# Delta rule block substitution on GpSimd, a new step order around it, and another timing model for the planned order

## The chip, the cores and the metric

One core of a Trainium2 chip runs the whole program in one launch. The metric is device time in microseconds (us), from the runs of the kernel on the chip; lower is better.

## What is computed

A two-layer model on 256 latent and 256 context tokens of width 1024. Each layer modulates its input, runs a mixer with three branches (a chunked delta rule, a gated linear attention and a differential attention), and a feed-forward part: dense in layer 0, a mixture of eight experts in layer 1. The change lies in the delta rule. Cut to it:

```python
decay = jnp.exp(jnp.where(incl, gc[..., :, None] - gc[..., None, :], -jnp.inf))
lmat = jnp.tril(jnp.einsum('bhnid,bhnjd->bhnij', kb, k) * decay, -1)
tinv = lax.linalg.triangular_solve(eye + lmat, eye, left_side=True, lower=True, unit_diagonal=True)
u = tinv @ (v * beta)
w = tinv @ (kb * jnp.exp(gc)[..., None])
# then a scan over the chunks: v_new = u - w @ s; s = s * gl + kg^T @ v_new
```

So for every head, direction and block of tokens a unit triangular matrix is inverted, and the scan over the chunks needs that inverse.

## The kernel before

The kernel is written tile by tile, in float32, with every large product made of three matmuls (lines 272 to 274) on operands split into two parts. A weight of 1 MB is fetched by SyncE into one of three buffers called raw; ScalarE casts its upper part (line 267), VectorE subtracts to get the lower part (line 268, two inputs from on-chip memory), and TensorE multiplies. Such a fetch with its two halves is one projection unit. Its two parts lie in a pool of six buffers (whl), its sums in three PSUM buffers (pm).

What runs in which order inside a mixer stands in PLAN, one line of short words per layer. The words that matter here: "pr" builds the triangular matrices U (a_prep), "iv" inverts them (a_inv and a_join), "sc" is the scan over the chunks (a_scan). "ga", "gb", "gc" with a number are that many gate projection units, stored to DRAM for later (gates_ahead); "za" is the two units of the output gate of the delta rule (z_ahead). "m" with a number runs so many steps of the modulation for later use (mod_unit): each fetches 1 MB of w_mod into raw and uses it in 16 small matmuls (line 348) without any work of VectorE or ScalarE on the weight. "qkB", "dec", "vB", "ha", "ma" are later steps of the other branches and of the merge.

Layer 1 works on half as many columns (256) in ga and za as layer 0 (512).

The inversion has three parts. First the diagonal blocks of 32 are gathered from U into one tile W and transposed (lines 638 to 648). Then comes the substitution: for c from 0 to 30 one multiplication (line 653) and one subtraction (line 655) on VectorE, over (31 - c) rows of (c + 1) elements on 128 partitions, each step reading what the step before wrote. At last the result is transposed back and put into U and a tile Q (lines 657 to 677), and a_join puts the blocks of 32 and 64 together with small matmuls (lines 699 to 728).

The word order in PLAN gives priorities, not the order on the engines. A planner in the tile framework works out an order for each engine from modelled durations, and every engine then takes its instructions strictly in that order.

Of the kernel before, what the change touches and what calls it, by code (L numbers as in the profile page):

```python
# [23 lines left out]
MOE_RAW = (1, 0, 0)  # L24
MOE_PART = 3
PRE = (7,)
PLAN = ("sm ap su pr iv ga4 m4 za sc m16 dec qkB gb1 ha ma vB gla qC kC m4 gc1 vC hb dif mb hc mc",
        "sm ap pr ga1 m8 iv sc za m6 ga3 m1 gc1 qkB dec vB ha ma gla qC kC m1 vC hb dif mb hc mc")
MOE_PRE = 9
MOE_AT = 0  # L30
PART = 512
# [165 lines left out]
class Prog:  # L197
# [430 lines left out]
    def a_inv(self, s):  # L628

        nc = self.nc  # L630
        U = s["U"]
        W1 = self.ch([2, 32, 32], "W1")
        W2 = self.ch([2, 32, 32], "W2")
        Dg, M, N, Y = W1[:, 0], W1[:, 1], W2[:, 0], W2[:, 1]
        nc.gpsimd.memset(Y, 0.0)
        nc.gpsimd.memset(Y.rearrange("p i j -> p (i j)")[:, 0:1024:33], 1.0)
        quad = [slice(b * 32, (b + 1) * 32) for b in range(4)]
        for d in range(2):
            for b, r in enumerate(quad):
                src, dst = U[d][r, :, r], Dg[r, :, 16 * d:16 * d + 16].rearrange("p i m -> p m i")  # L640
                if b % 2:
                    nc.vector.tensor_copy(dst, src)
                else:
                    nc.scalar.copy(dst, src)
        nc.vector.transpose(M, Dg)
        dmb = self.dmask[:, :, None].to_broadcast([128, 32, 32])
        nc.scalar.copy(N, M)
        nc.vector.copy_predicated(N, dmb, M.rearrange("p i j -> p j i"))
        for c in range(31):
            a, b = 31 - c, c + 1  # L650
            tmp = self.sm([512], "fs")
            tv = tmp[:, :a * b].rearrange("p (a b) -> p a b", a=a)
            nc.vector.tensor_mul(tv, N[:, c + 1:, c:c + 1].to_broadcast([128, a, b]),
                                 Y[:, c:c + 1, :b].to_broadcast([128, a, b]))
            nc.vector.tensor_sub(Y[:, c + 1:, :b], Y[:, c + 1:, :b], tv)
        Z, Ps, Qs = M, Dg, N
        nc.scalar.copy(Z, Y)
        nc.vector.copy_predicated(Z, dmb, Y.rearrange("p i j -> p j i"))
        nc.vector.transpose(Ps, Z)
        nc.vector.transpose(Qs, Z.rearrange("p i j -> p j i"))  # L660
        for d in range(2):
            for b, r in enumerate(quad):
                dst, src = U[d][r, :, r], Ps[r, :, 16 * d:16 * d + 16].rearrange("p i m -> p m i")
                if b % 2:
                    nc.vector.tensor_copy(dst, src)
                else:
                    nc.scalar.copy(dst, src)
        Q = W1.rearrange("p a i j -> p (a i j)").rearrange("p (d m j) -> p d m j", d=2, m=16)
        nc.gpsimd.memset(Q, 0.0)
        for d in range(2):  # L670
            for b, r in enumerate(quad):
                c = slice((b % 2) * 32, (b % 2) * 32 + 32)
                dst, src = Q[r, d, :, c], Qs[r, :, 16 * d:16 * d + 16].rearrange("p i m -> p m i")
                if b % 2:
                    nc.vector.tensor_copy(dst, src)
                else:
                    nc.scalar.copy(dst, src)
        self.a_join(U, Q)
# [761 lines left out]
    def mixer(self, l, H):  # L1440

        self.todo = self.mods(MOD_AHEAD[l], behind=0)
        T, m = {}, []
        gn = lambda n: self.P(f"gn{n}{l}") if n != "c" else self.A["gnc", l]
        zu = {"a": U_ZA, "b": U_RB, "c": None}
        for w in PLAN[l].split():
            if w == "su":
                self.setup2()
            elif w == "sm":
                self.small_proj(l, H)  # L1450
            elif w == "ap":
                self.a_proj(l, H)
            elif w == "pr":
                T["s"] = self.a_prep(l)
            elif w == "iv":
                self.a_inv(T["s"])
            elif w == "sc":
                T["oa"] = self.a_scan(l, T["s"])
            elif w == "qkB":
                T[w] = self.gla_qk(l, H)  # L1460
            elif w in ("vB", "vC"):
                T[w] = self.values(l, U_VB if w == "vB" else U_VC, H, w)
            elif w == "dec":
                self.gla_decays(l)
            elif w == "gla":
                T["ob"] = self.gla(l, T["qkB"], T["vB"])
            elif w == "qC":
                T[w] = self.diff_qk(l, H, w, U_QC, 256 * l, 0.125)
            elif w == "kC":
                T[w] = self.diff_qk(l, H, w, U_KC, 0, 1.0)  # L1470
            elif w == "dif":
                T["oc"] = self.diff(l, T["qC"], T["kC"], T["vC"])
            elif w[0] == "z":
                self.stashed[l, w] = self.z_ahead(l, zu[w[1]], H, gn(w[1]), w[1])
            elif w[0] == "g":
                self.gates_ahead(l, "abc".index(w[1]), H, int(w[2:] or 4))
            elif w[0] == "h":
                T["y" + w[1]] = self.head_out(l, T["o" + w[1]], gn(w[1]), H, zu[w[1]], w[1])
            elif w in ("ma", "mb", "mc"):
                first = not m  # L1480
                m = m or self.wide(l, "m")
                self.merge(l, "abc".index(w[1]), H, T["y" + w[1]], m, first)
            else:
                for _ in range(int(w[1:])):
                    next(self.todo, None)
        return m
# [86 lines left out]
```

## Time and profile before

| | us |
|---|---|
| median of 3 runs | 2604.94 (2601.87 to 2605.57) |
| profiled execution, its time | 2607.5 |
| profiled execution, its span | 2605.7 |
| TensorE busy | 2455.8 (94%) |
| VectorE busy | 1718.3 (66%) |
| ScalarE busy | 1417.3 (54%) |
| GpSimd busy | 87.6 (3%) |
| SyncE's transfers, busy share of the 16 DMA engines | 48.1% |

Engines in the rows below: PE is TensorE, PEld its weight loads, DVE VectorE, ACT ScalarE, POOL GpSimd, SP SyncE. Matmuls overlap, so the durations of single ones sum to more than the time that they take; the distance between starts is the time of one.

### The profile page before, as it was taken

Reading aid. Unit: us, or ns where it says so; the run is one execution under the profiler, and the core shown is the slowest. Engines: PE = TensorE matmul, PEld = TensorE weight load, DVE = VectorE, ACT = ScalarE, POOL = GpSimd, SP = SyncE. Lnnn points to the kernel's source line nnn. Section 1 sums busy time; section 2 is a strip of 40 time slices with the busy share of each in tenths; the row PEclk is TensorE's granted clock in tenths of the full one; section 3 lists DMA queues with packets and bytes.
Section 4 is the critical chain, followed back from the end, with each engine's and each line's share of the span. In section 5 each row is a group of like instructions: output and inputs, shape, how many; then the busy total and the mean of one; then the engine's idle time right before and its main releaser. Section 6 shows DMA issues by size and latency. Waiting matters only on the chain.

```text
span 2605.7 us, 35872 instructions
## 1 busy us (share of the span) xinstructions
PE 2455.8 (94%) x13712; PEld 1979.8 (76%) x13712; DVE 1718.3 (66%) x3130; ACT 1417.3 (54%) x2352; POOL 87.6 (3%) x216
## 2 busy tenths in 40 slices
PE   5998999999998999998979999998999999999997
PEld 3786777677677788886859878787878888878876
DVE  4675446655644533335686475767988888988987
ACT  3764343225553432334845432666878777777775
POOL 0000001110010000000000010010000000000000
PEclk8998999989999999998978999998999999999998
DMA  6323632022132223222273130246979899999994
GB/s 248 110 93 149 246 132 71 17 106 81 49 128 83 81 77 121 96 74 89 97 271 115 46 141 33 89 169 261 386 270 365 332 350 351 346 347 353 342 366 181
DMA packets 72707, 473.13 MB, mean 182 GB/s; under 512 B 8208, under 2 KB 10384, under 8 KB 19664
## 3 DMA queue, kind: packets, MB, share of 16 engines
q1 hardware_dynamic: 68208, 464.73, 48.1%
q10 hardware_dynamic: 4320, 6.03, 0.6%
q8 instruction: 110, 1.80, 0.3%
q14 instruction: 69, 0.57, 0.1%
HBM read 463.65 MB, written 7.08 MB: 181 GB/s over the span
## 4 chain that ended last, share of the span: by engine, by line
PE 85%; DVE 8%; ACT 4%; issue 2%; DMA 1%; SPq 0%; POOL 0%; ACTq 0%; DVEq 0%; POOLq 0%
PE pm L273 19%; PE pm L272 19%; PE pm L274 19%; PE y L274 3%; PE y L273 3%; PE y L272 3%; PE la L985 2%; PE pm L348 2%; PE pq L1052 1%; DVE ATb L987 1%; PE pm L844 1%; PE ob L996 1%; PE tp L1352 1%; DMA raw<-in_wmod_dram 1%; DVE zq L973 1%
## 5 line engine op out<-in xcount | busy, mean ns | idle before, releaser
L268 DVE TENSOR_TENSOR whl<-raw,whl 128x512 fp32r<-128x512 f32 (+2 forms) x490 | 331.2, 682 | 341.0 <-ACT whl L267 338.0
L272 PE MATMUL pm<-hh,whl 128*128 128x512 f32 (+2 forms) x1264 | 477.7, 380 | 13.0 <-ACT whl L267 6.6
L274 PE MATMUL pm<-hh,whl 128*128 128x512 f32 (+2 forms) x1264 | 467.7, 371 | 12.3 <-DVE whl L268 12.3
L267 ACT CAST whl<-raw 128x512 fp32r<-128x512 f32 (+2 forms) x490 | 289.8, 600 | 339.9 <-PE pm L274 268.7
L273 PE MATMUL pm<-hl,whl 128*128 128x512 f32 (+2 forms) x1264 | 470.9, 373 | 0.0
L268 DVE TENSOR_TENSOR wp<-rawc,wp 128x1024 fp32r<-128x1024 f32 x261 | 313.6, 1222 | 36.7 <-ACT wp L267 30.6
L272 PEld LDWEIGHTS pm<-hh,whl 128*128 128x128 f32 (+1 forms) x1264 | 244.8, 194 | 60.6 <-ACT whl L267 8.6
L274 PEld LDWEIGHTS pm<-hh,whl 128*128 128x128 f32 (+1 forms) x1264 | 243.5, 193 | 54.8 <-DVE whl L268 14.3
L267 ACT CAST wp<-rawc 128x1024 fp32r<-128x1024 f32 x261 | 268.1, 1051 | 21.1 <-PE y L274 11.5
L273 PEld LDWEIGHTS pm<-hl,whl 128*128 128x128 f32 (+1 forms) x1264 | 244.7, 194 | 42.6 <-issue 6.3
L268 DVE TENSOR_TENSOR wlo<-raw,whi 128x1024 fp32r<-128x1024 f32 x176 | 210.0, 1222 | 34.1 <-ACT whi L267 31.6
L273 PE MATMUL pm<-wlo,hg 128*128 128x512 f32 x530 | 211.8, 400 | 1.6 <-DVE wlo L268 1.4
L272 PE MATMUL pm<-whi,hg 128*128 128x512 f32 x530 | 211.2, 398 | 0.0
L274 PE MATMUL pm<-whi,hg 128*128 128x512 f32 x530 | 207.7, 392 | 0.0
L267 ACT CAST whi<-raw 128x1024 fp32r<-128x1024 f32 x176 | 179.0, 1052 | 13.2 <-PE pm L273 11.9
L273 PE MATMUL y<-wp,mt 128*128 128x512 f32 x348 | 135.4, 389 | 0.0
L274 PE MATMUL y<-wp,mt 128*128 128x512 f32 x348 | 135.3, 389 | 0.0
L273 PEld LDWEIGHTS pm<-wlo,hg 128*128 128x128 f32 x530 | 99.7, 188 | 34.6 <-DVE wlo L268 15.8
L272 PE MATMUL y<-wp,mt 128*128 128x512 f32 x348 | 120.1, 389 | 0.2 <-ACT mt L1354 0.2
L272 PEld LDWEIGHTS pm<-whi,hg 128*128 128x128 f32 x530 | 99.7, 188 | 20.9 <-ACT hg L1328 0.2
L274 PEld LDWEIGHTS pm<-whi,hg 128*128 128x128 f32 x530 | 99.7, 188 | 20.2
L268 DVE TENSOR_TENSOR wlo<-rawc,whi 128x1024 fp32r<-128x1024 f32 x91 | 110.9, 1219 | 1.9 <-ACT whi L267 1.3
(394 smaller groups left out, 4542.8 us busy)
## 6 DMA issues: line engine op xcount, KB each, us to landing
rawc<-in_m_dram SPq DMA_DIRECT2D x176, 1024.0 KB, 6.0
raw<-in_m_dram SPq DMA_DIRECT2D x88, 1024.0 KB, 7.4
raw<-in_win_dram SPq DMA_DIRECT2D x64, 1024.0 KB, 4.9
raw<-in_wmod_dram SPq DMA_DIRECT2D x40, 1024.0 KB, 5.0
raw<-in_f_dram SPq DMA_DIRECT2D x22, 1024.0 KB, 4.8
raw<-in_wo_dram SPq DMA_DIRECT2D x24, 512.0 KB, 3.7
raw<-in_f_dram SPq DMA_DIRECT2D x16, 704.0 KB, 4.0
rawc<-in_wmod_dram SPq DMA_DIRECT2D x8, 1024.0 KB, 16.9
```

Of the source, the lines that this page charges most:

```text
L267: self.nc.scalar.copy(hi, src)
L268: self.nc.vector.tensor_sub(lo, src, hi.bitcast(F32))
L272: mm(p, wh, ah, start=first, stop=False)
L273: mm(p, wh, al, start=False, stop=False)
L274: mm(p, wl, ah, start=False, stop=last)
L348: nc.tensor.matmul(p[j:j + 32, :256], self.cs[:, k, o:o + 32], w[:, k], start=i == 0 and k < 4, stop=i == n - 1 and k >= 4)
L844: nc.tensor.matmul(ps[:, :n], self.ones, sq[:, :n], start=True, stop=True)
L973: nc.vector.tensor_mul(FQ[hp][r, x, a].rearrange("p (n s) -> p n s", s=LEVELS[li]), side(Fj[:, x]), side(q[hp]))
L985: mm(p[:, x % 2, hp], FK[hp][:, x], FQ[hp][:, x], start=True, stop=True)
L987: nc.vector.copy_predicated(AT.rearrange("p h a (n t s) -> p (h a) n t s", t=2, s=s)[:, :, :, 1 - d], mk[:, None].to_broadcast([128, 4, 64 ...
L996: mm(o[:, hp], vB[:, tt, h * 128:(h + 1) * 128], AT[:, hp, a], start=True, stop=first)
L1052: mm(p[:, :nk], q[ms, h, cs], k[ms, h, :nk], start=True, stop=True)
```

## The change

The substitution's two instructions move from VectorE to GpSimd. The inversion is cut in two: a_inv ends with the substitution, and a new method a_blocks does the rest, from the copy that begins "Z" to the joins. A new word "jo" in PLAN calls it. PLAN is rewritten: in layer 0, "jo" stands behind "ga4 m4", with "za" behind it; in layer 1 "ga4 za m8" stands between "iv" and "jo", where "ga1 m8" stood ahead of "iv" and "za m6 ga3 m1" behind "sc", and the rest of the modulation ("m8") follows the scan; a last "m1" before "vC" goes. The tile context gets schedule_with_timeline_sim=True, so the planner works out its order with another timing model.

```diff
-PLAN = ("sm ap su pr iv ga4 m4 za sc m16 dec qkB gb1 ha ma vB gla qC kC m4 gc1 vC hb dif mb hc mc",
-        "sm ap pr ga1 m8 iv sc za m6 ga3 m1 gc1 qkB dec vB ha ma gla qC kC m1 vC hb dif mb hc mc")
+PLAN = ("sm ap su pr iv ga4 m4 jo za sc m16 dec qkB gb1 ha ma vB gla qC kC m4 gc1 vC hb dif mb hc mc",
+        "sm ap pr iv ga4 za m8 jo sc m8 gc1 qkB dec vB ha ma gla qC kC vC hb dif mb hc mc")
@@ a_inv
-            nc.vector.tensor_mul(tv, N[:, c + 1:, c:c + 1].to_broadcast([128, a, b]),
+            nc.gpsimd.tensor_mul(tv, N[:, c + 1:, c:c + 1].to_broadcast([128, a, b]),
                                  Y[:, c:c + 1, :b].to_broadcast([128, a, b]))
-            nc.vector.tensor_sub(Y[:, c + 1:, :b], Y[:, c + 1:, :b], tv)
-        Z, Ps, Qs = M, Dg, N
+            nc.gpsimd.tensor_sub(Y[:, c + 1:, :b], Y[:, c + 1:, :b], tv)
+        s["inv"] = W1, W2
+
+    def a_blocks(self, s):
+        U = s["U"]
+        W1, W2 = s["inv"]
+        Y = W2[:, 1]
+        Z, Ps, Qs = W1[:, 1], W1[:, 0], W2[:, 0]
         nc.scalar.copy(Z, Y)
         nc.vector.copy_predicated(Z, dmb, Y.rearrange("p i j -> p j i"))
@@ mixer
+            elif w == "jo":
+                self.a_blocks(T["s"])
@@ kernel
-    with tile.TileContext(nc) as tc:
+    with tile.TileContext(nc, schedule_with_timeline_sim=True) as tc:
```

## Rows read from the trace of the kernel before

**Rows 1.** The profile's page: span and instructions; busy time of each engine.

```profile
span 2605.7 us, 35872 instructions
...
PE 2455.8 (94%) x13712; PEld 1979.8 (76%) x13712; DVE 1718.3 (66%) x3130; ACT 1417.3 (54%) x2352; POOL 87.6 (3%) x216
```

**Rows 2.** Windows around both inversions: us, busy times, granted clock, DMA share, GB/s.

```profile
183.00:246.00 63.00, 49.99 (x652) 38.89 (x651) 44.30 (x100) 30.11 (x48) 1.81 (x1) 0.86 0.39 145
246.00:309.00 63.00, 62.23 (x615) 48.66 (x613) 25.22 (x54) 13.67 (x24) 0.00 (x0) 1.00 0.63 236
1302.00:1332.00 30.00, 22.77 (x225) 14.92 (x223) 23.85 (x79) 15.48 (x28) 0.00 (x0) 0.89 0.76 283
1302.00:1404.00 102.00, 80.92 (x1020) 65.54 (x1018) 81.47 (x201) 55.99 (x103) 1.81 (x1) 0.78 0.57 210
1404.00:1447.00 43.00, 43.00 (x362) 40.49 (x361) 19.75 (x40) 14.15 (x28) 0.00 (x0) 1.00 0.30 99
```

**Rows 3.** Windows of stages away from the inversions, the experts last.

```profile
400.00:580.00 180.00, 168.19 (x942) 128.91 (x940) 116.04 (x400) 51.50 (x118) 23.14 (x100) 0.94 0.17 63
620.00:740.00 120.00, 110.55 (x494) 75.97 (x493) 72.95 (x168) 66.92 (x147) 12.31 (x8) 0.97 0.21 75
1460.00:1600.00 140.00, 129.72 (x825) 105.69 (x825) 92.72 (x281) 59.72 (x138) 14.77 (x62) 0.99 0.25 87
1800.00:2580.00 780.00, 775.81 (x3550) 630.78 (x3550) 693.88 (x751) 591.47 (x738) 0.00 (x0) 1.00 0.90 341
```

**Rows 4.** Waits of PE, 1300 to 1420 us: total us, times, longest.

```profile
PE pm L348 <- DMA raw<-in_wmod_dram: 8.0, 6, 3.6
PE pm L274 <- DVE whl L268: 7.7, 2, 3.9
```

**Rows 5.** The substitution by source line: duration min/median/max ns, first and last start, forms.

```profile
L653 DVE TENSOR_TENSOR fs<-W x31: 192/360/425, 183.5 to 206.5; 128x31 f32<-128x31 f32 x2, 128x60 f32<-128x60 f32 x2, 128x87 f32<-128x87 f32 x2, 128x112 f32<-128x112 f32 x2
L655 DVE TENSOR_TENSOR W<-W,fs x31: 184/359/426, 183.8 to 207.2; 128x31 f32<-128x31 f32 x2, 128x60 f32<-128x60 f32 x2, 128x87 f32<-128x87 f32 x2, 128x112 f32<-128x112 f32 x2
L655 DVE TENSOR_TENSOR W<-W,fs x31: 183/359/424, 1339.2 to 1370.9; 128x31 f32<-128x31 f32 x2, 128x60 f32<-128x60 f32 x2, 128x87 f32<-128x87 f32 x2, 128x112 f32<-128x112 f32 x2
```

**Rows 6.** Two-input work on POOL: groups by shape, then single ones with DVE beside (timeline).

```profile
L1112 POOL TENSOR_TENSOR m<-m,sg 128x512 f32<-128x512 f32 x12 | 19.2, 1599 | 118.2 <-DVE sg L1111 92.5 <-DVE r L1059 19.7 <-DVE r L1054 6.0
L1112 POOL TENSOR_TENSOR m<-m,sg 128x256 f32<-128x256 f32 x14 | 13.5, 966 | 124.3 <-issue 63.1 <-DVE sg L1111 57.7 <-DVE r L1054 3.4
...
659.33 1.29 POOL L1112 TENSOR_TENSOR m<-m,sg 128x512 f32<-128x512 f32 x1 [19.71 <-DVE r L1059]
659.40 1.76 DVE L268 TENSOR_TENSOR whl<-raw,whl 128x512 fp32r<-128x512 f32 x1
...
1743.79 0.73 POOL L1112 TENSOR_TENSOR m<-m,sg 128x256 f32<-128x256 f32 x1 [5.47 <-DVE sg L1111]
```

**Rows 7.** Timeline of PE in layer 0: first join matmuls, first scan matmuls.

```profile
222.80 1.23 PE L699 MATMUL v<-W,U 32*32 32x32 f32 x116
...
246.35 1.05 PE L759 MATMUL V<-vtok,U 128*128 128x128 f32 x8
```

**Rows 8.** Layer 0: fetches behind "ga4", three modulation units on PE, one window of full DMA.

```profile
194.15 1.19 SPq L248 DMA_DIRECT2D raw<-in_win_dram  x2
200.18 0.33 SPq L248 DMA_DIRECT2D raw<-in_wmod_dram  x1
...
192.15 2.80 PE L348 MATMUL pm<-raw,cs 128*32 128x256 f32 x48
...
198.00:204.00 6.00, 3.69 (x22) 1.85 (x22) 5.52 (x15) 2.03 (x4) 0.00 (x0) 0.60 1.02 419
```

**Rows 9.** Pace of large matmuls: 512 columns (a window), 256 columns (two starts).

```profile
1060.00:1080.00 20.00, 20.00 (x90) 16.57 (x89) 8.16 (x12) 6.08 (x10) 0.00 (x0) 1.00 0.30 106
...
1341.17 0.28 PE L272 MATMUL pm<-hh,whl 128*128 128x256 f32 x1
1341.29 0.28 PE L273 MATMUL pm<-hl,whl 128*128 128x256 f32 x1
```

More of the change, by code (lines that the diff above doesn't have):

```diff
@@ L652, in a_inv @@
             tv = tmp[:, :a * b].rearrange("p (a b) -> p a b", a=a)
-            nc.vector.tensor_mul(tv, N[:, c + 1:, c:c + 1].to_broadcast([128, a, b]),
+            nc.gpsimd.tensor_mul(tv, N[:, c + 1:, c:c + 1].to_broadcast([128, a, b]),
                                  Y[:, c:c + 1, :b].to_broadcast([128, a, b]))
-            nc.vector.tensor_sub(Y[:, c + 1:, :b], Y[:, c + 1:, :b], tv)
-        Z, Ps, Qs = M, Dg, N
+            nc.gpsimd.tensor_sub(Y[:, c + 1:, :b], Y[:, c + 1:, :b], tv)
+        s["inv"] = W1, W2
+    def a_blocks(self, s):
+        nc = self.nc
+        U = s["U"]
+        W1, W2 = s["inv"]
+        quad = [slice(b * 32, (b + 1) * 32) for b in range(4)]
+        dmb = self.dmask[:, :, None].to_broadcast([128, 32, 32])
+        Y = W2[:, 1]
+        Z, Ps, Qs = W1[:, 1], W1[:, 0], W2[:, 0]
         nc.scalar.copy(Z, Y)
```

## The prediction

> **What bounds the kernel now.** I read the page first: PE is busy for 94% of the span and every other engine for much less [rows 1]. So time is to be had only where PE stands idle or runs slowly, and the next view is the windows over time. Around both inversions PE does both. In layer 0, from 183 to 246 us, it is busy 50.0 of 63 us (13.0 idle) at a mean granted clock of 0.86, which is the time at 2.4 GHz mixed with time at 1.2 GHz; 50.0 x 0.14 = 7 us more are lost to that. Together 20 us are lost. In layer 1, from 1302 to 1404, 21 us are idle and 80.9 x 0.22 = 18 us go to the clock: 39 us. Behind each, while the scan runs, PE is full at clock 1.00 [rows 2]. The third view is who PE waits for there: transfers of w_mod and the lower parts of weights (L268), which VectorE makes late because the substitution and the preparation stand ahead of them in its queue [rows 4]. So two things are late: DVE, and a DMA rate. A change here can win some part of 20 + 39 us, no more. Elsewhere the mixers' other branches leave 12, 9 and 10 us idle, and the experts 4 of 780 us [rows 3]: there is little to win there and much to lose.
>
> **The substitution on GpSimd.** Each layer has 31 steps of two instructions, together 2 x (sum of (31 - c)(c + 1)) = 2 x 5456 = 10,912 elements per partition. On VectorE it runs from 183.5 to 207.4 us in layer 0 (62 x 0.36 us by the medians, 22 us busy) and, mixed with other work, from 1338.5 to 1371.1 in layer 1 [rows 5]. On POOL the nearest rows are the merge's additions. The undisturbed ones take 1.29 us for 512 and 0.73 us for 256 elements, so 0.56 / 256 = 2.19 ns per element and 0.17 us per instruction; by that the chain takes 10,912 x 2.19 ns + 62 x 0.17 us = 34 us. The means, 1.599 and 0.966 us, give 2.47 ns and 0.33 us, so 27 + 21 = 48 us. Why the means are longer can be read too: a subtraction of a weight on VectorE that begins while an addition runs on POOL takes 1.76 us where its usual 0.69 would do, so the two engines hold each other up [rows 6]. In the changed kernel VectorE subtracts some 16 weight parts during the chain, and each can hold POOL up by about half its 0.69 us: 34 + 16 x 0.5 = 42 us. I take 42, with 34 and 48 as ends. That no row shows strided and broadcast operands on POOL is why 48 stays in the range. VectorE gets 22 us per layer back.
>
> The Trainium skill speaks against the step: "GPSIMD Engine Reference", section "Engine selection", sends elementwise work on two inputs to VectorE and calls GpSimd about twice as slow. By that factor 22 us become some 44 us (an estimate from that page), close to the sum from rows. What the rule leaves open is whether the lateness costs anything, and that is settled by what PE has to do meanwhile.
>
> **Layer 0.** The chain ends at 183.5 + 42 = 225.5 instead of 207.4. From there to the first full row of joins took 15.4 us, and from the joins to the scan 23.5 us, of which part was za's matmuls put between [rows 7]; without them I take 13. So joins begin at 241 and the scan at 254, 7.5 us later than before. What does PE do from 183 to 254? The end of ga4, 9 us (until the modulation at 192.15, as before). Then three waiting modulation units and a fourth, 4 us; the transfers for za are issued at 194 to 195 in either kernel and a 1 MB transfer needs 2.6 us at the 0.42 MB per us of the full window [rows 8], so about 7 us stay idle until 203. Now za can begin 4 us earlier, since its lower parts don't wait for the substitution: two units of 48 matmuls at 20 / 90 = 0.22 us [rows 9], 21 us, and 4 us for the clock to come back, until 228. From 228 to 241 only m16 is left, three units at hand and then one each 2.6 us for 1.0 us of PE: 6 us idle. Joins and scan start lose 3 more. Sum 7 + 4 + 6 + 3 = 20 us lost, as much as before: 0 gained. With a chain of 34 us it would be 5 gained, with 48 us 3 to 6 lost. What of m16 is done early, qkB's and gb1's 32 us of matmuls replace as cover of the scan.
>
> **Layer 1.** Ahead of "iv", ga4 takes the place of m8. Modulation needs nothing of VectorE; a gate unit needs four subtractions, 2.8 us, for 48 matmuls of 0.12 us = 5.6 us [rows 9]. While the preparation runs, VectorE has 6 of 30 us free [rows 2], so about two units fit and PE loses 4 us in place of 9.7 (7.2 idle, 2.5 clock). The chain starts at about 1335 (an estimate: 3 us earlier than now, with no modulation ahead of it) and ends at 1377; with the same 15.4 us and 11 us of joins the scan starts at 1404, as now. From 1332 the other four units of ga4 and za give PE 17 us at full pace (2 lost on the subtractions that POOL holds up). Then only modulation is left: about 36 us in which sixteen units at 2.6 us are fetched but give PE 17 us, so 19 us idle, and 4 us for the clock before gc1 and qkB arrive. Lost 4 + 2 + 19 + 4 = 29 against 39: 10 us gained. A chain of 34 us makes it 12, one of 48 us 7; 5 us either way for the guess of two units.
>
> **The order elsewhere.** Another timing model moves instructions in every stage. No row prices that, so it is bounded: below by half of the 31 us that the three mixed stretches leave idle, a gain of 15; above by the experts, which lose 0.5% now and might lose 3.5% (the mixed stretches lose 6.6 to 7.9% [rows 3]), a loss of 25. I take 0, since the experts' stretch is the longest and its loss is now the smallest.
>
> **Sum.** 0 + 10 + 0 from the profiled 2607.5 gives 2597.5; the median of the runs lies 2.6 below the profiled run, so **2595**.
>
> **The rivals.** *Slower: queues wait at the joins.* Engines take their instructions in planned order. If the planner holds POOL to be as fast as VectorE (24 us rather than 42), it puts the copy and the transposes behind the chain, and then the joins, 18 us too early, and VectorE, ScalarE and PE stand there with ready weights and za behind them. The price is the work that would have filled that time: about 13 us in layer 0 (za's end and six modulation units) and 9 in layer 1, so 2595 + 22 = 2617. It decides once the planned end lies more than about 10 us ahead of the real one. For it: today's order lets PE wait 7.7 us on weight parts that stand behind the substitution [rows 4], so the queues do block. Against it: the change brings a new timing model along, and a model that prices POOL long has no such loss.
>
> *No change: the idle time only moves.* Modulation stays bound by its transfers wherever it stands, and if only one gate unit fits into the preparation and the chain takes 48 us, layer 1 gains 2 and layer 0 loses 3: 2605.
>
> *Faster: the new order also helps elsewhere.* Chain of 34 us (5 + 12, and 5 for the units) and the 15 us: 2605 - 37 = 2568; half of the 15: 2575.
>
> **How the numbers follow.** My forecast has 0.42 (2584 to 2604 by itself), the waits at the joins 0.22, no change 0.14, the order helping 0.22. The range goes to the faster rival's far end, 2567, and upward to 2605 + 25 = 2630, which holds the slower rival too. A measurement of this kernel can tell some 0.2% (5 us) from no change. Of the forecast's chance 0.08 lies above 2600, so faster has 0.34 + 0.22 = 0.56, the same 0.20 (0.14 and 0.06), slower 0.24 (0.22 and 0.02).
>
> **What would show it.** The rows of lines 653 and 655 on POOL: first start to last end near 42 us in each layer; near 62 x 0.55 = 34 if VectorE doesn't disturb it. The windows 183 to 254 and 1302 to 1404: idle about 16 and 23 us. Weight parts of za made while the chain runs; if instead PE's wait before line 699 is one of over 8 us with line 272 behind it, the slower rival is right. The experts' 780 us should keep their length within 5 us; if they or the dense part move more, the order elsewhere decides, and my sum is wrong whatever the inversions show.

## The result and the profile after

The change makes the kernel slower: 2742.42 us (2738.34 to 2749.03, 4 runs) against 2604.07 (2601.87 to 2605.57) for the kernel before; the ratio is 1.0534, 95% interval 1.051 to 1.0559. That is 138 us more, on the other side of no change from the forecast and far outside its range. From about line 657 on, a line of the changed kernel has a number 10 higher than in the kernel before (the wait at 985 is now at 995).

The page of the changed kernel, its busy times and TensorE's granted clock in 40 slices:

```profile
span 2738.3 us, 36079 instructions
...
PE 2476.7 (90%) x13712; PEld 2022.1 (74%) x13712; DVE 1673.1 (61%) x3006; ACT 1420.5 (52%) x2352; POOL 156.7 (6%) x340
...
PE   6997889967969899999896889888999999999997
...
PEclk8998999966969999999996999799999999999998
```

Against [rows 1], TensorE runs the same 13712 matmuls and its busy time grew by 21 us, as more of them ran at the lower clock (the mean granted clock of the two executions is 0.962 and 0.928); its idle time grew from 150 to 262 us. VectorE was relieved by 45 us, GpSimd took on 69: the move itself did what it says. A slice is 68 us. The ninth, tenth and twelfth (548 to 684 and 753 to 821 us) have TensorE busy for 6, 7 and 6 tenths at a clock of 0.6: that is where layer 0's gated linear and differential attention run.

Windows of the changed kernel: both inversions, layer 1's substitution by itself, one stretch in the middle of layer 0's substitution, six windows at the end of layer 0's gated linear attention, and the experts (columns: length, busy time of PE, PEld, DVE, ACT and POOL with instruction counts, granted clock, DMA share, GB/s):

```profile
183.00:254.00 71.00, 50.27 (x673) 36.11 (x673) 28.94 (x41) 32.71 (x49) 37.13 (x63) 0.82 0.62 230
1400.00:1500.00 100.00, 76.05 (x848) 56.66 (x846) 53.57 (x123) 49.34 (x90) 34.08 (x63) 0.76 0.65 237
...
1437.40:1476.00 38.60, 24.77 (x208) 9.82 (x204) 1.60 (x8) 2.16 (x4) 32.28 (x62) 0.59 0.96 355
...
200.00:220.00 20.00, 20.00 (x87) 16.47 (x85) 6.88 (x8) 7.49 (x13) 18.04 (x26) 0.96 0.44 158
...
540.00:560.00 20.00, 15.44 (x107) 12.94 (x106) 12.11 (x38) 5.62 (x12) 2.02 (x10) 0.91 0.09 27
560.00:580.00 20.00, 13.78 (x52) 9.71 (x51) 7.72 (x27) 2.62 (x7) 2.02 (x8) 0.67 0.00 0
580.00:600.00 20.00, 12.40 (x43) 10.51 (x43) 10.53 (x40) 2.46 (x6) 2.55 (x11) 0.50 0.01 2
600.00:620.00 20.00, 13.83 (x56) 10.32 (x54) 10.15 (x44) 3.63 (x8) 2.61 (x12) 0.59 0.00 0
620.00:640.00 20.00, 13.50 (x42) 10.43 (x43) 8.33 (x30) 1.96 (x4) 2.12 (x9) 0.50 0.00 0
640.00:660.00 20.00, 15.37 (x51) 11.51 (x50) 7.88 (x26) 2.48 (x7) 1.01 (x4) 0.50 0.01 1
...
1920.00:2700.00 780.00, 767.99 (x3554) 631.91 (x3554) 682.89 (x747) 595.80 (x739) 0.00 (x0) 1.00 0.90 342
```

Read the line from 200 first: while GpSimd works on the substitution of layer 0 (18.04 of 20 us), TensorE is full, so the move is hidden there. In layer 1 it is not: from 1437 to 1476 us TensorE has 24.77 of 38.6 us at a clock of 0.59, the DMA engines are full (0.96), and its only work is modulation that waits for its transfers. Then the six windows from 540: no engine is full, next to nothing is fetched (DMA share 0.00 to 0.09), and from 560 us on TensorE works two thirds of the time (68.9 of 100 us) at a granted clock of 0.50 to 0.67; 0.50 is its lower level of 1.2 GHz. The same stage had 168 of 180 us at 0.94 before (400 to 580 us in [rows 3]). The experts' 780 us lose 12.0 instead of 4.2.

Waits of TensorE over the whole changed kernel (total us, times, longest) and the substitution by source line:

```profile
PE la L995 <- DVE Fe L986: 38.3, 16, 3.5
PE pm L348 <- DMA raw<-in_wmod_dram: 25.9, 15, 4.1
...
PE tp L1075 <- DVE e L1072: 22.8, 8, 4.3
```

```profile
L653 POOL TENSOR_TENSOR fs<-W x62: 238/547/1089, 190.7 to 1473.9; 128x31 f32<-128x31 f32 x4, 128x60 f32<-128x60 f32 x4, 128x87 f32<-128x87 f32 x4, 128x112 f32<-128x112 f32 x4
```

In the kernel before, the same three waits were these:

```profile
PE pm L348 <- DMA raw<-in_wmod_dram: 11.8, 7, 3.7
PE tp L1065 <- DVE e L1062: 6.8, 11, 1.1
...
PE la L985 <- DVE Fe L976: 6.4, 13, 1.0
```

The waits for Fe and for e belong to the gated linear attention and to the differential attention, whose code the change doesn't touch. What is new there is the planner's order; the experiments below take it by itself.

Where the time went can be followed by landmarks, the first or last start of one instruction each (us):

| landmark | before | after |
|---|---|---|
| first addition of scan outputs, layer 0 | 264.9 | 281.6 |
| first addition of gated linear attention outputs | 460.6 | 503.9 |
| first copy of differential attention outputs | 642.7 | 709.0 |
| last residual addition of the mixer, layer 0 | 835.6 | 923.6 |
| last addition of the dense part, layer 0 | 1211.1 | 1299.1 |
| last addition of scan outputs, layer 1 | 1449.8 | 1579.1 |
| last copy of differential attention outputs, layer 1 | 1700.2 | 1837.7 |

17 us are lost by the first scan, 27 from there to the second landmark, 23 to the third, 22 to the end of layer 0's mixer, none in the dense part, 41 to the end of layer 1's scan, and 8 to the last; in the profiled runs 5 come back behind it.

### The profile page after: what moved, and what is told of

Its sections match the earlier page's. It is cut to its first block, busy times and chain, and to the rows that moved or that the text cites. A ratio compares the mean times of both kernels' runs of the same rounds, so it can differ in the third digit from the quotient of the medians.

```text
span 2738.3 us, 36079 instructions
## 1 busy us (share of the span) xinstructions
PE 2476.7 (90%) x13712; PEld 2022.1 (74%) x13712; DVE 1673.1 (61%) x3006; ACT 1420.5 (52%) x2352; POOL 156.7 (6%) x340
## 5 line engine op out<-in xcount | busy, mean ns | idle before, releaser
L268 DVE TENSOR_TENSOR whl<-raw,whl 128x512 fp32r<-128x512 f32 (+2 forms) x490 | 337.1, 696 | 368.1 <-ACT whl L267 364.5
```

The costliest lines, as they stand in the source:

```text
L268: self.nc.vector.tensor_sub(lo, src, hi.bitcast(F32))
```

## Experiments

Times are medians; ratios are against runs of the kernel before on the same chip. "The model" is schedule_with_timeline_sim=True.

**The change in its parts.** Theory A: the model's order costs the time. Rival B: the substitution on GpSimd does. Four kernels take the parts one by one.

The kernel before with the model alone:

```diff
-    with tile.TileContext(nc) as tc:
+    with tile.TileContext(nc, schedule_with_timeline_sim=True) as tc:
```

> The kernel before with nothing changed but the timing model of the planner; substitution on VectorE and plan as before. Theory A (the order of the new timing model carries the loss): 2690 to 2740 us, with the linear attention of layer 0 ending in a stretch of over 60 us in which PE is half busy at a granted clock near 0.5. Rival B (the plan and the later joins carry it): within 10 us of the kernel before, 2595 to 2615 us.

Measured: 2725.89 (2724.93 to 2731.28), ratio 1.0467 (1.0442 to 1.0492): 119 of the 138 us with nothing moved to GpSimd. Its windows have the same hole; this is the stretch 500 to 640 us:

```profile
500.00:640.00 140.00, 109.18 (x552) 90.72 (x551) 68.91 (x240) 32.18 (x70) 14.79 (x64) 0.71 0.11 38
```

And so are the waits of TensorE for VectorE:

```profile
PE la L985 <- DVE Fe L976: 36.2, 17, 3.5
...
PE tp L1065 <- DVE e L1062: 23.8, 8, 4.3
```

The changed kernel without the model:

```diff
-    with tile.TileContext(nc, schedule_with_timeline_sim=True) as tc:
+    with tile.TileContext(nc) as tc:
```

> The changed kernel with the old timing model: substitution on GpSimd, joins as a step of their own, new plan. Theory A: 2580 to 2610 us, as the sum of the prediction without its term for the order (2595). Rival B (plan and later joins): 2700 us or more. A third reading, that the old model misjudges GpSimd and the queues wait at the joins: 2615 to 2640 us, with a wait of over 8 us ahead of the join matmuls.

The kernel before with only the two instructions on GpSimd, PLAN and model as before:

```diff
-            nc.vector.tensor_mul(tv, ...)
-            nc.vector.tensor_sub(Y[:, c + 1:, :b], ...)
+            nc.gpsimd.tensor_mul(tv, ...)
+            nc.gpsimd.tensor_sub(Y[:, c + 1:, :b], ...)
```

> The kernel before with only the substitution's two instructions moved to GpSimd; plan and timing model as before, joins directly behind the substitution. Theory A: within 15 us of the kernel before (the chain ends some 10 us later than on VectorE, VectorE is free meanwhile). Rival (queues wait at the joins): 2620 us or more.

Measured: 2645.05, ratio 1.015 (1.012 to 1.018), and 2645.46, ratio 1.0144 (1.0118 to 1.017). So GpSimd costs 38 us under the old model. One window of the first, then its wait of ScalarE; one window of the second, then its wait of TensorE in layer 1:

```profile
200.00:220.00 20.00, 0.00 (x0) 0.00 (x0) 0.00 (x0) 1.02 (x2) 16.52 (x32) 0.50 0.23 95
```

```profile
ACT W L667 <- POOL W L655: 52.6, 2, 26.3
```

```profile
200.00:220.00 20.00, 0.19 (x4) 0.00 (x0) 0.00 (x0) 0.00 (x0) 17.49 (x33) 0.50 0.31 129
```

```profile
PE v L699 <- ACT W L677: 28.4, 1, 28.4
```

For 20 us next to nothing runs but GpSimd. In the first kernel ScalarE has reached the first copy of the joins (line 667) and waits 26 us for it. In the second, layer 1, TensorE itself stands 28.4 us at the joins' first matmul, the sign that the prediction named. This is its "slower" rival, in the kernels without the model. In the changed kernel no queue stands like that: TensorE had 20.00 of 20 us in layer 0, and in layer 1 it waited for transfers.

The new PLAN and the split of a_inv alone, with the substitution on VectorE and the old model, against the changed kernel:

```diff
-            nc.gpsimd.tensor_mul(tv, ...)
-            nc.gpsimd.tensor_sub(Y[:, c + 1:, :b], ...)
+            nc.vector.tensor_mul(tv, ...)
+            nc.vector.tensor_sub(Y[:, c + 1:, :b], ...)
...
-    with tile.TileContext(nc, schedule_with_timeline_sim=True) as tc:
+    with tile.TileContext(nc) as tc:
```

> The kernel before with the new plan and the joins as a step of their own, the substitution still on VectorE, old timing model. Theory A: 2590 to 2615 us. Rival B (the plan carries the loss): 2700 us or more, since layer 1 has no gate units left for its scan.

Measured: 2609.21, ratio 1.0015 (1.0003 to 1.0027). PLAN costs some 3 us (1 to 7 by the interval). So A carries 119 us. B is worth 38 without the model and, by difference, some 16 with it (138 less 119 for the model and 3 for PLAN).

**What in the model's order?** First theory: independent projections are used up too early. In the changed kernel the three projections of the differential attention were done by 546 us, and the gated linear attention ran alone until 658.

The kernel with the model, with these projections held back behind steps of the gated linear attention:

```diff
+            at = {"qC": (0, 1, 0), "kC": (1, 0, 0), "m4": (1, 1, 0), "gc1": (1, 1, 0), "vC": (1, 1, 1)}.get(w)
+            with self.tc.issue_after(self.step[at]) if at else nullcontext():
                 self.item(l, w, H, T, m, gn, zu)
```

> The kernel before with the timing model alone (2726 us), with layer 0's independent projections held back on TensorE's queue to the pace of the gated linear attention: those of the differential attention's q behind its second step, of k behind the third, the modulation and gate behind the fourth, of v behind the fourth's second direction (in the kernel before they stood like that; with the model all of them were used up by 546 us, and from there to 640 us TensorE ran half busy at a clock of 0.50 to 0.59). Theory 'the model's order spends the independent work too early': the stretch 500 to 640 us has TensorE at 17 of 20 us or more per window and a clock over 0.8, and 25 to 35 us come back: 2690 to 2702 us. Rival 'the model's order of the recurrence itself is slower, on VectorE and ScalarE, and the projections have no part in it': the low windows only move, to 430 to 540 us or behind it, and the time stays within 10 us of 2726.

The same, and each part of layer 0's second merge behind one query tile of the differential attention:

```diff
         for pr in range(4):
+            at = l == 0 and j == 1 and self.dstep[l, pr]
+            with self.tc.issue_after(at) if at else nullcontext():
```

> As the kernel with the projections held back, and with the four parts of layer 0's second merge held back as well, one behind each query tile of the differential attention (with the model, TensorE was at 11 to 14 of 20 us at a clock of 0.54 to 0.74 from 760 to 820 us). Theory 'spent too early': another 15 to 20 us come back, 2670 to 2687 us. Rival 'the recurrence and the softmax themselves': no more than 5 us beside the kernel with the projections alone.

The changed kernel with both:

> The changed kernel (2742 us) with both held back in layer 0, the projections behind the gated linear attention's steps and the second merge's parts behind the query tiles. Theory 'spent too early': 40 to 55 us come back, 2687 to 2702 us, since its low windows (540 to 660, 760 to 820 us) are those of the kernel with the model alone. Rival 'the recurrence and the softmax themselves': within 10 us of 2742.

Measured: 2720.46 (ratio 1.0445, 1.0427 to 1.0462), 2710.96 (1.0402, 1.0377 to 1.0428), 2737.78 (1.051, 1.0492 to 1.0527). By the loss against the kernel before on the same chip 3, 13 and 5 us came back, where 25 to 55 were expected. The theory fell: the holes moved, as its rival said. The timeline of TensorE in the first of them shows how a step now runs (line 987 is 985 before; start us, length, engine, line, what, and in brackets idle time with its releaser):

```profile
495.38 1.19 PE L987 MATMUL la<-zq,Fe 128*128 128x128 f32 x4 [1.61 <-DVE Fe L978]
...
497.65 2.38 PE L987 MATMUL la<-zq,Fe 128*128 128x128 f32 x8
503.71 3.36 PE L987 MATMUL la<-zq,Fe 128*128 128x128 f32 x12 [3.68 <-DVE Fe L978]
508.73 0.77 PE L998 MATMUL ob<-ATb,vB 128*128 128x128 f32 x2 [1.66 <-DVE ATb L989]
...
517.08 0.63 PE L272 MATMUL pm<-hh,whl 128*128 128x512 f32 x1
```

And in the kernel before, at the same place in a step:

```profile
472.91 0.39 PE L274 MATMUL pm<-hh,whl 128*128 128x512 f32 x1
473.35 0.68 PE L985 MATMUL la<-zq,Fe 128*128 128x128 f32 x4
...
474.57 0.39 PE L272 MATMUL pm<-hh,whl 128*128 128x512 f32 x1
```

From 484 to 517 us no projection matmul (lines 272 to 274) runs; TensorE waits for VectorE, and its clock is 0.50, so that four products of 128 columns take 1.19 instead of 0.68 us. In the kernel before a step is shot through with projection matmuls. Counting, from the timelines of TensorE, the times of over 3 us in layer 0's gated linear attention (from its first decay matmul to the end of its last output) from the end of one projection matmul to the start of the next: before 8 of them, together 65 us, the longest 22; with the model 3, together 137, the longest 112; with the projections held back 6, together 140, the longest 50; in the changed kernel 3, together 137, the longest 112.

Second theory: blocks instead of weaving. The kernel with the model, with 144 groups of three projection matmuls woven by hand into the eight steps, and as a control the kernel before with the same:

```diff
+                        with self.pump(5):
                             for x, li in enumerate(ls):
...
+                        with self.pump(3):
                             for a, r in enumerate(rows):
```

Here pump(n) traces n groups behind TensorE's last instruction, and what stands under it is queued behind them.

> The kernel before with the timing model (2726 us), with layer 0's gated linear attention and its independent projections (q, k, v of the differential attention, one gate: 144 groups of three matmuls) woven together by hand: five groups are queued on TensorE between the matmuls that make the decay factors and the products that wait for them, three between the products and the outputs, in each of its eight steps. With the projections only held back by steps, the model's order still issued a step's own matmuls in one block (484 to 516 us: 32 us for one step, TensorE at a clock of 0.52 with holes of 1 to 4 us behind VectorE) and the projections in another; in the kernel before a step with projections in its holes took 23 us (466 to 489) at full clock. Theory 'blocks instead of weaving: the holes and the half clock that they bring': the stretch 380 to 640 us has TensorE at 17 of 20 or more and the clock at 0.9 or more, and 30 to 45 us come back, 2681 to 2696 us. Rival 'the model's order of the recurrence on VectorE and ScalarE': the holes stay beside the woven projections, 2710 us or more.

> The kernel before, with the planner's old model, and the same weaving by hand in layer 0's gated linear attention. By the weaving theory the old model wove by itself: nothing to win, 2600 to 2615 us. If the weaving by hand is itself a gain or a loss of more than 12 us, the reading of the kernel with the model has to be corrected by that.

Measured: 2770.72 (ratio 1.0633, 1.06 to 1.0666) and 2650.97 (1.017, 1.0138 to 1.0202). My fixed weave costs 46 us by itself, so by the rule set down ahead the reading is corrected by that: between the two kernels lie 120 us, as much as the model costs without the weave (119). Windows of the first and of the control, 380 to 680 us:

```profile
380.00:680.00 300.00, 251.29 (x1357) 207.68 (x1356) 141.74 (x447) 70.71 (x156) 24.12 (x104) 0.84 0.18 64
```

```profile
380.00:680.00 300.00, 270.63 (x1600) 223.53 (x1599) 165.59 (x507) 98.37 (x221) 25.90 (x105) 0.95 0.19 68
```

In these 300 us TensorE gets 1357 instructions done with the model, and 1600 without; but the control ends its gated linear attention at 612 us and goes on to other work, the first kernel only at 676. From its first decay matmul to that end the stage takes 313 us with the model and 264 without. So with equal weave the model still costs 49 us there: the place of the projections is not all of it, and something else in the order has a part.

**Whose order?** That question can be put without a theory of the order. The kernel is planned once with the old model, and TensorE's instructions are then held in just that order (an edge from each to the next) while the model plans the other engines; and the complement.

```diff
+    _, per = build(False)
+    nc, _ = build(True, [per[e] for e in ENGINES])   # each list: o[n] issued behind o[n-1]
...
+ENGINES = ('PE',)      # the complement: ('DVE', 'Activation', 'Pool', 'SP')
```

> The kernel before with the timing model (2726 us), but TensorE's instructions are held in the very order that they have in the kernel before; the model plans VectorE, ScalarE, GpSimd and the fetches around that. Theory 'TensorE's order decides' (projections and recurrence in the wrong turn): 2604 to 2630 us. Rival 'the order on VectorE and ScalarE decides' (each waits behind other work while TensorE stands): 2690 us or more. Between: both have a part.

> The complement: VectorE, ScalarE, GpSimd and the fetches are held in the order of the kernel before, and the model plans TensorE alone. Theory 'TensorE's order decides': 2680 us or more. Rival 'the order on VectorE and ScalarE decides': 2604 to 2640 us.

Measured: 2638.84 (ratio 1.0134, 1.0109 to 1.0159) and 2792.0 (1.0714, 1.0697 to 1.0732). TensorE's order brings back 85 of the 119 us; 34 stay, more than expected. Without TensorE's order, the old order of all others is of no use, and worse than none (+68). In the gated linear attention of the first one:

```profile
355.00:600.00 245.00, 215.70 (x1198) 169.50 (x1198) 144.97 (x458) 72.86 (x160) 25.80 (x112) 0.94 0.20 74
```

The stage takes 248 us (353 to 601), against 235 before and 289 with the model alone; its times without a projection are 9, together 68 us, the longest 24. Of the 34 us that stay, 18 are lost by the first copy of differential attention outputs in layer 0, 4 from there to the end of layer 1's scan, and 15 to the last copy; 4 come back behind it. TensorE, in its old order, waits more for the two other engines:

```profile
PE la L985 <- DVE Fe L976: 27.4, 26, 1.9
...
PE v L699 <- ACT W L677: 17.0, 2, 9.6
```

Before, these two were 6.4 and 1.2 us. So what is left agrees with a worse order on VectorE and ScalarE.

**What makes the queues stand still without the model?** First try: cover is missing. The joins are queued on TensorE, VectorE and ScalarE behind the last gate (layer 0) or behind za (layer 1):

```diff
+                for i in pins: es.enter_context(self.tc.issue_after(i))
                 self.a_blocks(T["s"])
...
+            if w == ("ga4", "za")[l]: pins = [last instruction of each engine]
```

> The changed kernel with the planner's old model (2645 us, 15 of whose first 20 us after the chain's start at 200 us had TensorE, VectorE and ScalarE all waiting for GpSimd), and one thing more: everything of the joins on TensorE, VectorE and ScalarE is queued behind the last instruction of the gates (layer 0) or of the delta rule's z (layer 1) on the same engine, so that no queue can reach the joins before some 35 to 42 us of projections have been issued. Theory 'the standstill is the whole price of GpSimd under the old model': TensorE is full from 200 to 220 us and from 1360 to 1390 us, 30 to 45 us come back, 2597 to 2615 us, about the kernel before or a little under it. Rival 'the chain on GpSimd costs elsewhere too (its instructions hold VectorE up, the order around it is worse)': TensorE is full there, but the time stays over 2625 us.

Measured: 2640.44, ratio 1.0141 (1.0124 to 1.0159); TensorE 0.89 of 20 us from 200 to 220. Nothing was cured, since the pins held the joins behind the wrong thing. I first read it as gates issued too early, and held the cover itself back, on TensorE behind the last matmul ahead of the chain ("[" to "]" in PLAN), with the joins behind the cover:

```diff
+PLAN = ("... iv ga4 [ za gb1 ] m4 jo sc m16 dec qkB ha ...",
+        "... iv ga2 m4 [ ga2 za gc1 ] m4 jo sc m8 qkB ...")
```

> The changed kernel's parts with the planner's old model (2645 us), with cover that is queued on TensorE between the chain on GpSimd and the joins: behind the last matmul ahead of the chain stand the delta rule's z and a gate of the gated linear attention (layer 0: some 32 us of projections), or two gates, z and another gate (layer 1: some 27 us), and everything of the joins on TensorE, VectorE and ScalarE stands behind those. With the joins queued behind the gates alone the standstill stayed (TensorE 0.89 of 20 us from 200 to 220), because the gates were issued ahead of the chain. Theory 'the standstill is the whole price of GpSimd under the old model': TensorE is nearly full through both chains and 30 to 45 us come back, 2595 to 2615 us. Rival 'work held for the chain is missing ahead of it or behind it': the holes only move, to the preparation ahead of the chain or the scan behind it, and the time is over 2625 us.

Measured: 2606.29 (2601.82 to 2611.16, 10 runs), ratio 1.0004 (0.9989 to 1.002): the 38 us came back. Layer 0's chain is covered, layer 1's not (windows), and the timeline of layer 1 tells what the wait is:

```profile
200.00:220.00 20.00, 20.00 (x90) 16.57 (x89) 6.07 (x7) 9.14 (x15) 17.88 (x28) 1.00 0.44 151
...
1360.00:1380.00 20.00, 0.42 (x4) 0.00 (x0) 7.26 (x7) 5.24 (x5) 9.80 (x22) 0.50 0.30 114
```

```profile
1371.48 1.04 ACT L667 COPY W<-W 128x1024 f32<-128x1024 f32 x1 [17.88 <-POOL W L655]
...
1380.06 0.37 ACT L356 COPY modr<-pm 128x256 f32<-128x256 f32 x1
...
1380.48 1.02 PE L359 MATMUL pm<-cstt,modr 128*128 128x8 f32 x4 [20.06 <-ACT modr L356]
```

A copy of 0.37 us that has nothing to do with the inversion, the modulation's (line 356), stands on ScalarE behind the joins' first copy (line 667). That one waits for GpSimd, and TensorE waits 20.1 us for the small copy, with all its other work behind. The timeline of TensorE in the changed kernel without the model has the same wait in layer 0:

```profile
197.05 1.07 PE L348 MATMUL pm<-raw,cs 128*32 128x256 f32 x16 [3.72 <-DMA raw<-in_wmod_dram]
220.35 1.02 PE L359 MATMUL pm<-cstt,modr 128*128 128x8 f32 x4 [22.23 <-ACT modr L356]
```

So in these two places TensorE stood neither at the joins' matmuls nor for want of work, but at a place in a queue. The direct trial holds nothing back for the chain, and only queues the joins behind all that PLAN sets ahead of them, za and the modulation included:

```diff
+PLAN = ("... iv ga4 m4 za } jo sc m16 ...", "... iv ga4 za m8 } jo sc m8 ...")
...
+            if w == "}": pins = [last instruction of TensorE, VectorE, ScalarE]
```

> The changed kernel with the planner's old model (2645 us), with the joins on TensorE, VectorE and ScalarE queued behind all that PLAN sets ahead of them, and za set ahead of them in layer 0 as well: nothing is held for the chain. In the standstill of layer 0 the last thing that TensorE waits for, 22 us, is the modulation's sum (line 359), whose input is a copy of 0.36 us on ScalarE (line 356) that stands behind the joins' first copy (line 667), which waits for GpSimd; it was so in the kernel with the joins behind the gates too, since the modulation comes after the gates. Theory 'that one copy and the casts of za's weights behind the joins' copy make the standstill': TensorE is at 17 of 20 us or more from 200 to 220, no wait of line 359 is over 5 us in either layer, and 2600 to 2615 us. Rival 'cover has to be held back for the chain': TensorE runs dry all the same, because the gates are issued ahead of the chain, and the time stays over 2625 us.

And with one gate more ahead of the joins in each layer:

```diff
+PLAN = ("... iv ga4 m4 za gb1 } jo sc m16 dec qkB ha ...", "... iv ga4 za m8 gc1 } jo sc m8 qkB ...")
```

> As the kernel with the joins behind everything ahead of them, and one gate more ahead of them in each layer (gb1 in layer 0, gc1 in layer 1: some 11 and 6 us of projections). If TensorE still runs dry before the chain's end with less, each us of it is worth one: 2590 to 2605 us. If the joins then start late behind the gate, as in the kernels with more cover, 2610 to 2630 us.

Measured: 2615.68 (2606.71 to 2622.24, 6 runs), ratio 1.0048 (1.0031 to 1.0064), and 2604.89 (2600.15 to 2607.91, 10 runs), ratio 0.9998 (0.9988 to 1.0008). One window of the first:

```profile
200.00:220.00 20.00, 18.64 (x75) 15.09 (x76) 9.95 (x12) 8.56 (x15) 17.89 (x28) 0.88 0.61 227
```

Against the kernel before on the same chip, 27 of the 38 us came back with the copy and za ahead of the joins (the edit moves both, so the copy's share by itself is not shown), and 11 more with a gate of cover. The longest wait of line 359 in these stretches fell from 22.2 and 26.0 us to 0.5. What is left in the first kernel is a wait of 10.3 us at the joins' first matmul in layer 1, 0.2 with the gate more; its time lies just above what was expected, so some cover is needed as well.

Two kernels went on from the one with held cover. With one gate more in layer 0 and two in layer 1 inside the brackets ("[ za gb2 ]" and "[ ga4 za gc1 ]"):

> The kernel with cover behind the chain on GpSimd and the planner's old model (2606 us) with more of it: another gate in layer 0 (some 11 us of projections) and two more in layer 1 (some 12 us). With less, TensorE still had 12.16 of 20 us from 220 to 240 at a clock of 0.72, and 0.42 of 20 from 1360 to 1380 at 0.50. Theory 'each us of cover up to the chain's length saves one': 7 to 10 us in layer 0 and 12 to 18 in layer 1 come back, 2578 to 2590 us, faster than the kernel before. Rival 'the work is taken from the preparation and the later stages, which then lack it': 2600 us or more.

And with the cover split, the joins' layout steps on VectorE and ScalarE behind "]", their matmuls behind "}" ("[ za gb1 ] gb1 }" and "[ ga3 za ] gc1 gb1 }"):

> The kernel with cover behind the chain on GpSimd (2606 us), with the cover split in two: the joins' layout steps on VectorE and ScalarE stand behind z and one gate (layer 0) or three gates and z (layer 1), about the chain's length, so that they start when the chain ends; the joins' matmuls stand behind one or two gates more, which run on TensorE during those steps (12 us from the chain's end, 224, to the first join's matmul, 236; when the same gate stood ahead of the layout steps too, they only came 12 us later, and 2627 us were measured). In layer 1 the modulation stands ahead of the chain or behind the joins, since its copy on ScalarE stood behind the joins' first copy and TensorE waited 20.1 us for it. Theory 'cover to the right length on each queue': 8 to 10 us in layer 0 and 12 to 18 in layer 1 come back, 2578 to 2590 us. Rival 'work given to the chain is missing in the later stages': 2600 to 2615 us.

Measured: 2627.25 (ratio 1.0082, 1.0065 to 1.0099) and 2631.97 (1.0101, 1.0067 to 1.0136): both worse than less cover. In the first the joins of layer 0 start 12 us later (first matmul of line 709 at 250.9 us, 238.5 with less cover). In the second the wait on ScalarE is back under another name, a gate's sigmoid behind the joins' copy; a row of its waits of TensorE, 1300 to 1440 us:

```profile
PE pm L272 <- ACT sg L402: 15.9, 2, 14.7
```

No variant with GpSimd beat the kernel before; two equal it.

## Why the prediction was wrong

**The step that failed is "the order elsewhere".** It took 0 with -15 and +25 as bounds. The kernel with the model alone puts it at +119. The bounds came from the wrong stages: I held the experts to be the most exposed, since their stretch is the longest and loses the least, and allowed them 3.5%. Over 780 us they lost 8 more. The mixers, which I counted only as a possible gain, lost 88 us in layer 0 alone (835.6 to 923.6 us at its last residual addition). What I had not weighed is that a loss can feed itself there: a step of the gated linear attention waits for VectorE several times, and where no woven projections keep TensorE busy meanwhile it idles, the clock goes to 1.2 GHz, and the step's own matmuls take longer as well (1.19 for 0.68 us). The timelines show that much; that missing weave is the whole cause is not shown. The last sentence of the prediction, on the experts and the dense part, was right in what it concluded and wrong in its sign: the experts' matmuls grew from 780 to 785 us from first to last, the dense part kept its 375.5 us, and the mixers, which that sentence doesn't name, moved.

**The bound** was right as far as it went: TensorE's idle time (112 us more) and its longer busy time (21 us more) are the whole difference of the two profiled executions, and there was little to win elsewhere and much to lose. "Much to lose" was written down and then priced at 25 us.

**The substitution on GpSimd** came out near its price, in part by luck. I took 42 us, between 34 and 48. In the changed kernel it ran from 190.7 to 230.8 us, 40 us, and from 1437.4 to 1474.5, 37 us. Without VectorE's subtractions of weight parts beside it (layer 1 here, layer 0 in the kernels that stand still) it takes 37, not 34: my sum left out the 0.08 us from one instruction to the next. The disturbance was set too high. I multiplied 16 parts by 0.5 us, where half of 0.69 is 0.35; in layer 0 only eight parts came beside the chain and added 3 us. With projections as cover 12 and 16 parts added 5 and 6 (41.9 and 42.8 us), some 0.4 each. The 1.29 us that I took as undisturbed is no such row either, since a subtraction begins 0.07 us behind it [rows 6]. The Trainium skill, "GPSIMD Engine Reference", section "Engine selection", has GpSimd some two times slower on two inputs; here 37 to 43 us stand against the 24 of [rows 5], 1.5 to 1.8 times, so the page was right in direction and a little high in size. No arrangement of the move gained.

**Layer 0 and layer 1.** Losses of 20 and 29 us were forecast, in 183 to 254 us and around the second inversion. Measured: 20.7 idle and 9 for the clock (50.3 x 0.18) in the first, 24 and 18 (76.05 x 0.24) in the stretch 1400 to 1500. So 72 where I had 49 and the kernel before 59. In layer 0 the chain began 7 us later than I had it. In layer 1 the chain itself was read well: 13.8 idle and 10 for the clock (24.77 x 0.41), 24 against the 23 that I gave to modulation bound by its transfers. One of them took 3.0 us at the 355 GB/s of that window; I had 2.6, and my own 0.42 MB per us would have made it 2.5. The clock was the term that was set too low, 4 us in each layer where it took 9 and, in the chain of layer 1 alone, 10. The gain of 10 became a loss of 13. In the kernel with the model alone the same two stretches lose 58, 14 less than with GpSimd and the new PLAN, which agrees with the 16 us of the experiments.

**The rivals.** "Queues wait at the joins" named a real mechanism, with a price of 22 us. Without the model it is there and costs 38, because what it blocks is more than I had counted: not za's weights on VectorE, but a small copy on ScalarE by which TensorE stands for 22 us in layer 0 and 26 in layer 1. With the model no such loss appeared: the longest wait for that copy is 3.7 us in the changed kernel. That this is so because the model prices GpSimd's work long, as its counter-argument had it, no trace shows. "No change" and "faster, the order also helps" fell. I looked at the model only for what it would do to the joins; every other stage was planned with it too.

**What stays open.** That TensorE's order costs most of it is shown (85 of 119 us), and the rest agrees with the order of VectorE and ScalarE. That the core of TensorE's order is missing weave rests on the counts and on the stretch that shortens when the old order is put back; my own weave did not repair it, so which instruction stands wrong is not settled. Nor is what the model prices differently, which no trace shows. The 41 us between the dense part and the end of layer 1's scan are not taken apart either: the kernel with the model alone loses 29 of them.

## What to carry to other kernels

A switch that replans every queue is a change to every stage: price it by the stage that is bound by latency and kept full only by woven work, not by the stage that is longest, and measure it alone before anything is combined with it. When a step moves to a slower engine, ask what each in-order queue holds behind the first instruction that waits for it; a copy of 0.4 us there could stop TensorE for 20 us here, and queueing the waiting instruction behind it and za gave 27 of the 38 us back. More cover than that ended even with the kernel before at best, and with still more the joins started late and the time grew.

## What the runs showed of the hardware

- A chain of dependent instructions on GpSimd with nothing beside it spends 32.2 us busy in 37.0 us from first start to last end, 62 instructions: 0.08 us between one and the next (layer 0 of the changed kernel without the model; spans on GpSimd are rough). With VectorE subtracting 8 to 16 weight parts beside it, the same instructions are busy for 35 us (the changed kernel, layer 0) to 38 (the kernel with held cover, layer 1).
- TensorE's granted clock was 0.50 to 0.67 in the windows of the changed kernel from 560 us on, in which it was busy for 12 to 15 of 20 us with gaps of up to 3.5 us, and 0.94 in [rows 3], where the same steps were woven with projections. Four products of 128 columns took 1.20 us there (1.19 with the projections held back) against 0.68.
